# High and low parts of the activations interleaved in SBUF, and moved 256 bytes from the weights' place

## The chip, the cores and the metric

The kernel runs on one core of one Trainium2 chip. The metric is the device time of one execution in microseconds (us). A result here is the median of several executions, shown with the lowest and the highest. Beside them stands one profiled execution, in which the hardware recorded when each instruction began. Its records are read through views: a page with the totals, groups of instructions by line of the kernel, a timeline, and sums over stretches of time.

Five engines work side by side and wait for each other through semaphores. TensorE multiplies (PE in the profile, and PEld for the loads of its stationary operand), VectorE is DVE, ScalarE is ACT, GpSimd is POOL, and SyncE (SP) issues most of the DMAs.

## What is computed

The reference is one decoder block over 256 tokens with a model width of 2048, in float32:

```python
xn = _rms_norm(h, mix_norm_w[l])
proj = xn @ w_in[l]
p_ssm, p_gdn, p_gate = jnp.split(proj, [SSM_PROJ, SSM_PROJ + GDN_PROJ], axis=-1)
y_ssm = _ssd_branch(p_ssm, ...) @ w_branch_ssm[l]
y_gdn = _gdn_branch(p_gdn, ...) @ w_branch_gdn[l]
gates = jax.nn.sigmoid(p_gate.reshape(b_, t, N_BRANCHES, D_MODEL) + gate_b[l])
mixed = gates[:, :, 0] * y_ssm + gates[:, :, 1] * y_gdn
h = h + mixed @ w_out[l]
hn = _rms_norm(h, ffn_norm_w[l])
h = h + _peer_ffn(hn, peer_w_q[l], peer_sub_keys[l], peer_u[l], peer_v[l])
return _rms_norm(h, final_norm_w)
```

The two mixers are a Mamba-2 scan (ssm) and a gated delta net (gdn). The last sub-layer scores 16,384 single-neuron experts and keeps 16 for each of 8 heads. The kernel evaluates all the experts and weights them with a gate that is zero for those not chosen.

## The kernel before

All the large products have one form. The activations are the **stationary** operand (128 rows of the inner dimension by 128 tokens) and the weights are the **moving** operand (128 rows by mostly 512 columns). To keep float32 accuracy, each operand is cut into a high part in the type float32r and a low part that holds the rest. One product is then three matmuls: high by high, high by low, and low by high.

**The weights.** `Stream` loads 512 KB units (`raw`, 128 x 1024 floats, four buffers of 4096 bytes a partition) through SyncE. `split` (lines 100 to 111) cuts a unit with one activation on ACT (`whi`, line 107) and one subtraction on DVE (`wlo`, line 108), with three buffers each of 4096 bytes. There are 1129 units, used in a fixed order.

**The products.** `product` (lines 291 to 308) walks over the inner chunks k of a unit and the two token blocks tb. For each it issues lines 302, 303 and 304: `xa` by `h_`, `xa` by `l_`, `xb` by `h_`, where `xa` and `xb` are the high and the low part of the activations. After each k, `bg.step` may emit a step of a background chain (convolutions, scans, transposes, gates) between the matmuls. `mixing` (lines 1015 to 1027) does the same for the expert values, with lines 1021, 1022, 1027 and 1024.

**The activations.** They stand in these tiles, where a high and a low tile have the same shape:

- `xh`, `xl` (lines 243, 244): the normed input, for the input projection;
- `yh`, `yl` (lines 526, 624): the output of a mixer, for the branch projections;
- `mh`, `ml` (lines 729, 730): the merged branches, for the output projection;
- `hh`, `hl` (lines 788, 789): the second normed input, for the query product and the expert activations;
- `cf` (line 1009): the coefficients of the experts, for the mixing of the values, in two halves that are refilled in turn by `coef` (lines 990 to 996).

`split_t` (lines 248 to 250) writes a high part on ACT and the low part on DVE. In every one of these tiles the 256 tokens of a chunk are contiguous, so that a stationary operand reads 128 neighbouring floats (512 bytes) on each partition.

**The place in memory.** The pool `act` has four slots of 16,384 bytes on each partition, named `t16`, in which `xs`, `xh`, `xl`, `accg`, `aux`, `accs`, `h`, `hh`, `hl`, `keys`, the gate stages, `cf` and `fw` follow one another. Right behind it lie the four raw buffers, and behind them the three of `whi` and the three of `wlo`. Then come the pools of the stages, of which the last, `peer`, holds two `m16` slots: first `mh` and `ml`, later the two gate tiles `gg`.

Of the kernel before, what the change touches and what calls it, by code (L numbers as in the profile page):

```python
# [8 lines left out]
F = mybir.dt.float32  # L9
# [20 lines left out]
def in_proj_tiles():  # L30
    """Column ranges of w_in for each streamed tile, in the order in which they are used."""
    z, xs, b, c = 0, 4096, 8192, 9216
    dt = 10240
    gq, gk, gv = GDN_BASE, GDN_BASE + 2048, GDN_BASE + 4096
    gz = GDN_BASE + 8192
    bt = GDN_BASE + 12288

    def bc(g):
        return [(b + 128 * g, 128), (c + 128 * g, 128)]

    t = {"small": bc(0) + [(dt, 64), (bt, 16), (bt + 16, 16)]}
    for h in range(NH):
        t["qkv", h] = [(gq + 128 * h, 128), (gk + 128 * h, 128), (gv + 256 * h, 256)]
    for j in range(NH // 2):
        t["gz", j] = [(gz + 512 * j, 512)]
    for g in range(NG):
        t["sx", g] = [(xs + 512 * g, 512)]
        t["sz", g] = [(z + 512 * g, 512)]
    for g in (1, 3, 5):
        t["bc", g] = bc(g) + bc(g + 1)  # L50
    t["bc", 7] = bc(7)
    for i in range(2):
        for n in range(4):
            t["gate", i, n] = [(GATE_BASE + 2048 * i + 512 * n, 512)]
    return t


def schedule():
    """The order in which the weight tiles of the mixing sub-layer are used."""
    o = [("in", ("gz", 0)), ("in", "small")]  # L60
    for j in range(NH // 2):
        o.append(("in", ("qkv", 2 * j)))
        if j > 1:
            o.append(("br", "gdn", j - 2))
        o.append(("in", ("qkv", 2 * j + 1)))
        if j != 6:
            o.append(("in", ("gz", min(j + 1, 7))))
    o += [("in", ("gate", 1, 0)), ("in", ("gate", 1, 1)), ("br", "gdn", NH // 2 - 2),
          ("in", ("gate", 1, 2)), ("br", "gdn", NH // 2 - 1)]
    for g in range(NG):  # L70
        if g % 2:
            o.append(("in", ("bc", g)))
        o += [("in", ("sx", g)), ("in", ("sz", g))]
        if g:
            o.append(("br", "ssm", g - 1))
    o += [("in", ("gate", 1, 3)), ("in", ("gate", 0, 0)), ("in", ("gate", 0, 1)),
          ("br", "ssm", NG - 1), ("in", ("gate", 0, 2)), ("in", ("gate", 0, 3))]
    return o


class Stream:
    """Weights from DRAM: raw units ahead of their use, each cut into two float32r parts."""

# [37 lines left out]
class Background:  # L121
    """Chains of small steps that run between the large products."""

# [35 lines left out]
def block(ctx, tc, nc, I, out, dbg=None):  # L159
    cp = ctx.enter_context(tc.tile_pool(name="consts", bufs=1))  # L160
    T16 = ctx.enter_context(tc.tile_pool(name="act", bufs=4))
    big = ctx.enter_context(tc.tile_pool(name="big", bufs=4, space=PSUM))
# [3 lines left out]

# [1 line left out]
    order = schedule()  # L168
# [25 lines left out]

# [1 line left out]
    def big_tile():  # L196
# [20 lines left out]

    xs = T16.tile([128, 2, D], F, name="t16")
    strm = Stream(tc, nc, ctx, units, 4, 3)
# [15 lines left out]

# [1 line left out]
    def row_scale(r, m, parts):  # L237
        """m = sum of squares / D + eps, r = m ** -1/2, [128, 2] each"""
        V.tensor_reduce(m, parts, axis=mybir.AxisListType.X, op=OP.add)
        V.tensor_scalar(m, m, 1.0 / D, EPS, op0=OP.mult, op1=OP.add)  # L240
        power(r, m, 0, 2)

    xh = T16.tile([128, 16, T], FR, name="t16")
    xl = T16.tile([128, 16, T], FR, name="t16")
    sqp = cp.tile([128, 2, 4], F, name="sqp")
# [43 lines left out]

# [1 line left out]
    def product(lhs, nk, w, kpu, hook=None):  # L291
        """per token block, in PSUM: the sum over k chunks of lhs(k, tb) x streamed weights"""
        ps = [big_tile() for _ in range(2)]
        for u in range(nk // kpu):
            hi, lo = strm.next()
            for a in range(kpu):
                k = u * kpu + a
                h_, l_ = hi[:, a * w:(a + 1) * w], lo[:, a * w:(a + 1) * w]
                for tb in range(2):
                    xa, xb = lhs(k, tb)  # L300
                    o = ps[tb][:, :w]
                    PE.matmul(o, xa, h_, start=k == 0, stop=False)  # L302
                    PE.matmul(o, xa, l_, start=False, stop=False)  # L303
                    PE.matmul(o, xb, h_, start=False, stop=k == nk - 1)  # L304
                if hook:
                    hook(k)
                bg.step(1)
        return ps
# [3 lines left out]

# [1 line left out]
    raw0 = cp.tile([128, 2, 352], F, name="raw0")  # L314
# [8 lines left out]
    def small_gen():  # L323
# [10 lines left out]
        V.tensor_scalar(beta, beta, 0.5, 0.5, op0=OP.mult, op1=OP.add)  # L334
        # log(1 + e) = 2 atanh(e / (2 + e))
        V.tensor_scalar(s_, e_, 2.0, None, op0=OP.add)
# [29 lines left out]

# [1 line left out]
    mix = ExitStack()  # L368

    def conv(items, w, bias):  # L370
        """items of (dst, src psum [128, 256], chunk); dst gets half the causal convolution (+ bias)"""
        for dst, src, c in items:
            S.activation(dst, src, AF.Identity, scale=w[:, c, 3:4], bias=0.0 if bias is None else bias[:, c:c + 1])  # L373
        for k in (2, 1, 0):
            s = 3 - k
            for dst, src, c in items:
                V.scalar_tensor_tensor(dst[:, s:], src[:, :T - s], w[:, c, k:k + 1], dst[:, s:], op0=OP.mult, op1=OP.add)  # L377

    def conv_silu(pool, src, nch, chunk_of, w, bias, dst):
        """src(tb, i) [128 t, 128 c] in SBUF; dst [128 c, nch, 256] = silu(conv)"""  # L380
        y = pool.tile([128, 4, T], F, name="t4", bufs=NT4[0])
# [15 lines left out]
    def gdn_gen(h, pt, zg, yref):  # L397
# [127 lines left out]
        if not yref:  # L525
            yref += [mx.tile([128, 4, T], FR, name=n, bufs=1) for n in ("yh", "yl")]
        yh, yl = yref
# [15 lines left out]
    def ssm_gen(g, pt, bce, zg, yref):  # L543
# [78 lines left out]
        while g and ("ssm", g - 1) not in merged:  # L622
            yield
        yref += [mx.tile([128, 4, T], FR, name=n, bufs=1) for n in ("yh", "yl")]
        yh, yl = yref
# [97 lines left out]
    for o in order:  # L723
        if o[0] == "br":
            branch(o[1], o[2])
            if o[1:] == ("ssm", NG - 1):
                mix.close()
                pp = ctx.enter_context(tc.tile_pool(name="peer", bufs=1))
                mh = pp.tile([128, 16, T], FR, name="m16", bufs=2)
                ml = pp.tile([128, 16, T], FR, name="m16", bufs=2)  # L730
            continue
# [53 lines left out]

# [1 line left out]
    h = T16.tile([128, 2, D], F, name="t16")  # L787
    hh = T16.tile([128, 16, T], FR, name="t16")
    hl = T16.tile([128, 16, T], FR, name="t16")
    sqh = cp.tile([128, 2, 4], F, name="sqh")  # L790
# [36 lines left out]

# [1 line left out]
    tv, i1f, i2f = (pp.tile([128, 2, 8, 16], F, name=n) for n in ("tv", "i1f", "i2f"))  # L829
# [132 lines left out]

# [1 line left out]
    def act_gen(u, ps):  # L964
# [13 lines left out]

# [1 line left out]
    def gate_load(qg, half):  # L980
        ks = slice(16 * half, 16 * half + 16)
        src = gdr[ks, :, qg * 16:qg * 16 + 16, :].rearrange("k p i t -> p k i t")
        S.dma_start(gg[qg % 2][:, ks], src)

# [5 lines left out]
    def coef(qd, hq):  # L990
        g_ = gg[(qd // 4) % 2][:, :, (qd % 4) * 4:(qd % 4) * 4 + 4, :].rearrange("p k i t -> p i k t")
        h4 = hq.rearrange("p i (k t) -> p i k t", k=32)
        V.tensor_tensor(h4, h4, g_, op=OP.mult)
        hi, lo = cf[:, 0, qd % 2], cf[:, 1, qd % 2]
        S.activation(hi, hq, AF.Copy)
        V.tensor_tensor(lo, hq, hi.bitcast(F), op=OP.subtract)

    for u in range(32):
        if u == 31:
            bg.drain([ge])  # L1000
            gg = [pp.tile([128, 32, 16, 8], F, name="m16", bufs=2) for _ in range(2)]
            gate_load(0, 0)
# [5 lines left out]
        if u == 30:  # L1008
            cf = T16.tile([128, 2, 2, 4, T], FR, name="t16")
    acc = [[big_tile() for _ in range(2)] for _ in range(2)]  # L1010
# [4 lines left out]
    def mixing(i2, hv, cut, tb):  # L1015
        hi, lo = cut
        a, b = (cf[:, s, (i2 // 4) % 2, i2 % 4, tb * 128:(tb + 1) * 128] for s in range(2))
        for n in range(2):
# [33 lines left out]
    for i2, hv in v_order:  # L1052
        qd = i2 // 4
        if hv == 0:
# [6 lines left out]
            if i2 == 120:  # L1061
                fw = T16.tile([128, D], F, name="t16")
                G.dma_start(fw, bc_ap(I["fnw"], D))
# [15 lines left out]

# [1 line left out]
    residual(1, 0)  # L1081
# [77 lines left out]
```

## Time and profile before

| what | value |
|---|---|
| median of 3 runs | 3481.92 us (3481.53 to 3482.91) |
| span of the profiled execution, first to last instruction | 3480.8 us |
| PE busy | 3449.5 us (99%), 16598 matmuls |
| PEld busy | 2849.9 us (82%), 16598 loads |
| DVE busy | 2308.9 us (66%) |
| ACT busy | 1762.0 us (51%) |
| POOL busy | 318.3 us (9%) |
| moved by DMA | 682.36 MB, 196 GB/s in the mean |

The page gives the profiled execution by its span; it has no separate time with what lies around it, and the span is 1.1 us under the median. PE counts as busy from the start of a matmul to its modelled end. Matmuls overlap one another, so how fast PE works is read from the distance between starts, not from the busy share or from the length of one matmul.

### The profile page before, as it was taken

Reading aid. Unit: us, or ns where it says so; the run is one execution under the profiler, and the core shown is the slowest. Engines: PE = TensorE matmul, PEld = TensorE weight load, DVE = VectorE, ACT = ScalarE, POOL = GpSimd, SP = SyncE. Lnnn points to the kernel's source line nnn. Section 1 sums busy time; section 2 is a strip of 40 time slices with the busy share of each in tenths; the row PEclk is TensorE's granted clock in tenths of the full one; section 3 lists DMA queues with packets and bytes.
Section 4 is the critical chain, followed back from the end, with each engine's and each line's share of the span. In section 5 each row is a group of like instructions: output and inputs, shape, how many; then the busy total and the mean of one; then the engine's idle time right before and its main releaser. Section 6 shows DMA issues by size and latency. Waiting matters only on the chain.

```text
span 3480.8 us, 44496 instructions
## 1 busy us (share of the span) xinstructions
PE 3449.5 (99%) x16598; PEld 2849.9 (82%) x16598; DVE 2308.9 (66%) x3262; ACT 1762.0 (51%) x2420; POOL 318.3 (9%) x262
## 2 busy tenths in 40 slices
PE   9999999999999999999999999999999999999998
PEld 7888888888878888888888888888888788888886
DVE  6675766666667677777665667768887455555555
ACT  5565555555445554544445444446666444444444
POOL 0111111111100000000000000003443000000000
PEclk9999999999999999999999999999999999999999
DMA  7544444544555555555566566666777777777774
GB/s 258 158 138 152 151 145 142 154 150 147 157 166 183 192 187 182 185 178 182 189 203 200 172 199 208 206 210 224 236 241 242 253 245 242 241 242 243 241 234 163
DMA packets 233720, 682.36 MB, mean 196 GB/s; under 512 B 21072, under 2 KB 72480, under 8 KB 233248
## 3 DMA queue, kind: packets, MB, share of 16 engines
q1 hardware_dynamic: 164960, 594.03, 53.7%
q10 hardware_dynamic: 67616, 81.31, 6.8%
q0 software_dynamic: 928, 4.19, 0.4%
q8 instruction: 130, 2.13, 0.3%
q14 instruction: 86, 0.70, 0.1%
HBM read 643.71 MB, written 35.73 MB: 195 GB/s over the span
## 4 chain that ended last, share of the span: by engine, by line
PE 69%; DVE 1%; ACT 1%; issue 0%; ACTq 0%; DMA 0%; POOL 0%; POOLq 0%; DVEq 0%
PE acc L302 15%; PE acc L304 15%; PE acc L303 15%; PE acc L1022 3%; PE acc L1021 3%; PE acc L1027 3%; PE pst L1027 3%; PE pst L1021 3%; PE pst L1022 3%; PE pst L234 2%; PE pst L948 1%; PE pst L594 1%; DVE wlo L108 0%; ACT whi L107 0%; PE pst L598 0%
## 5 line engine op out<-in xcount | busy, mean ns | idle before, releaser
L108 DVE TENSOR_TENSOR wlo<-raw,whi 128x1024 fp32r<-128x1024 f32 (+1 forms) x1129 | 1439.9, 1282 | 916.2 <-ACT whi L107 906.1
L107 ACT ACTIVATE whi<-raw 128x1024 fp32r<-128x1024 f32 (+1 forms) x1129 | 1184.9, 1053 | 850.9 <-PE acc L304 440.5
L302 PE MATMUL acc<-whi,t 128*128 128x512 f32 (+2 forms) x2848 | 1168.8, 410 | 9.7 <-ACT whi L107 9.7
L304 PE MATMUL acc<-whi,t 128*128 128x512 f32 (+2 forms) x2848 | 1110.3, 390 | 0.0
L303 PE MATMUL acc<-wlo,t 128*128 128x512 f32 (+2 forms) x2848 | 1108.0, 389 | 1.8 <-DVE wlo L108 1.8
L304 PEld LDWEIGHTS acc<-whi,t 128*128 128x128 f32 x2848 | 535.6, 188 | 115.7
L302 PEld LDWEIGHTS acc<-whi,t 128*128 128x128 f32 x2848 | 536.7, 188 | 105.1 <-ACT whi L107 10.2
L303 PEld LDWEIGHTS acc<-wlo,t 128*128 128x128 f32 x2848 | 537.6, 189 | 99.2 <-DVE wlo L108 3.9
L302 PE MATMUL acc<-whi,yh 128*128 128x512 f32 x512 | 216.8, 423 | 2.8 <-ACT yh L249 2.8
L304 PE MATMUL acc<-whi,yl 128*128 128x512 f32 x512 | 202.9, 396 | 0.0
L303 PE MATMUL acc<-wlo,yh 128*128 128x512 f32 x512 | 202.4, 395 | 0.0
L1022 PE MATMUL pst<-wlo,t 128*128 128x512 f32 x512 | 200.0, 391 | 2.1 <-DVE wlo L108 2.1
L1021 PE MATMUL pst<-whi,t 128*128 128x512 f32 x512 | 200.1, 391 | 0.0
L1021 PE MATMUL acc<-whi,t 128*128 128x512 f32 x512 | 199.2, 389 | 0.0
L1022 PE MATMUL acc<-wlo,t 128*128 128x512 f32 x512 | 199.2, 389 | 0.0
L931 POOL TENSOR_TENSOR b<-ob,gp 128x1024 f16<-128x1024 f16 x64 | 141.0, 2203 | 625.6 <-DVE ob L930 625.6
L1027 PE MATMUL pst<-whi,t 128*128 128x512 f32 x508 | 156.8, 390 | 0.0
L1027 PE MATMUL acc<-whi,t 128*128 128x512 f32 x508 | 156.4, 389 | 0.0
L377 DVE SCALAR_TENSOR_TENSOR t<-pst,cols,t 128x255 f32<-128x255 f32 x336 | 135.9, 474 | 23.7 <-ACT t L373 23.3
L302 PEld LDWEIGHTS acc<-whi,yh 128*128 128x128 f32 x512 | 96.8, 189 | 23.2 <-ACT yh L249 3.2
L304 PEld LDWEIGHTS acc<-whi,yl 128*128 128x128 f32 x512 | 96.5, 188 | 23.3 <-DVE yl L250 0.2
L1022 PEld LDWEIGHTS pst<-wlo,t 128*128 128x128 f32 x512 | 96.5, 188 | 22.5 <-DVE wlo L108 2.4
(267 smaller groups left out, 3325.8 us busy)
## 6 DMA issues: line engine op xcount, KB each, us to landing
raw<-w_in SPq DMA_DIRECT2D x408, 512.0 KB, 3.6
raw<-u SPq DMA_DIRECT2D x256, 512.0 KB, 4.0
raw<-v SPq DMA_DIRECT2D x256, 512.0 KB, 4.4
raw<-w_gdn SPq DMA_DIRECT2D x64, 512.0 KB, 3.5
raw<-w_ssm SPq DMA_DIRECT2D x64, 512.0 KB, 4.4
raw<-w_out SPq DMA_DIRECT2D x32, 512.0 KB, 3.8
raw<-w_q SPq DMA_DIRECT2D x32, 512.0 KB, 3.6
hdr<-ht ACTq DMA_DIRECT2D x32, 512.0 KB, 4.9
```

The source lines that it names most:

```text
L107: self.nc.scalar.activation(hi[:, s], t[:, s], AF.Copy)
L108: self.nc.vector.tensor_tensor(lo[:, s], t[:, s], hi[:, s].bitcast(F), op=OP.subtract)
L234: PE.transpose(dst, src, ident)
L302: PE.matmul(o, xa, h_, start=k == 0, stop=False)
L303: PE.matmul(o, xa, l_, start=False, stop=False)
L304: PE.matmul(o, xb, h_, start=False, stop=k == nk - 1)
L377: V.scalar_tensor_tensor(dst[:, s:], src[:, :T - s], w[:, c, k:k + 1], dst[:, s:], op0=OP.mult, op1=OP.add)
L594: PE.matmul(p[:, i * 64:(i + 1) * 64], sc[:, i, :], xdt[:, c, i, :], start=True, stop=True)
L931: G.tensor_tensor(b2, ob[:, None, :, :].to_broadcast([128, 2, 4, 128]), gp[:, :, ts, None].to_broadcast([128, 2, 4, 128]), op=OP.mult)
L1021: PE.matmul(o_, a, hi[:, s], start=i2 == 0, stop=False)
L1022: PE.matmul(o_, a, lo[:, s], start=False, stop=False)
L1027: PE.matmul(acc[tb][2 * hv + n], b, hi[:, n * 512:(n + 1) * 512], start=False, stop=False)
```

## The change

The high and the low part of an activation no longer have a tile each. They share one, in which element 2t is the high part of token t and element 2t + 1 the low part. A stationary operand so reads 128 floats with a step of two, over 1024 bytes. `parts` gives the two views.

The pool `act` now has two `t16` slots and one larger tile, `pair`, for `xh`/`xl`, later `hh`/`hl`, and at the end `fw`. `pair` is 64 floats (256 bytes) longer than its contents, and `xs` makes the two `t16` slots 16 floats (64 bytes) longer each. The products, the order of the work and the number of instructions are as before. Docstrings and comments that the diff also removes are left out here.

```diff
-    T16 = ctx.enter_context(tc.tile_pool(name="act", bufs=4))
+    T16 = ctx.enter_context(tc.tile_pool(name="act", bufs=2))
+
+    def pair_tile(dt):
+
+        t = T16.tile([128, 2 * 16 * T + 64], dt, name="pair", bufs=1)
+        return t
+
+    def parts(t, k):
+        t = t[:, :2 * k * T].rearrange("p (k t s) -> p k t s", k=k, s=2)
+        return t[:, :, :, 0], t[:, :, :, 1]
+
...
-    xs = T16.tile([128, 2, D], F, name="t16")
+    xs = T16.tile([128, 2 * D + 16], F, name="t16")[:, :2 * D].rearrange("p (a b) -> p a b", a=2)
...
-    xh = T16.tile([128, 16, T], FR, name="t16")
-    xl = T16.tile([128, 16, T], FR, name="t16")
+    xh, xl = parts(pair_tile(FR), 16)
...
-            yref += [mx.tile([128, 4, T], FR, name=n, bufs=1) for n in ("yh", "yl")]
+            yref += parts(mx.tile([128, 8 * T], FR, name="yhl", bufs=1), 4)
...
-                mh = pp.tile([128, 16, T], FR, name="m16", bufs=2)
-                ml = pp.tile([128, 16, T], FR, name="m16", bufs=2)
+                mh, ml = parts(pp.tile([128, 32 * T], FR, name="m32"), 16)
...
-    hh = T16.tile([128, 16, T], FR, name="t16")
-    hl = T16.tile([128, 16, T], FR, name="t16")
+    hh, hl = parts(pair_tile(FR), 16)
...
-        S.dma_start(gg[qg % 2][:, ks], src)
+        S.dma_start(gg[:, qg % 2, ks], src)
...
-        hi, lo = cf[:, 0, qd % 2], cf[:, 1, qd % 2]
+        hi, lo = (c[:, 4 * (qd % 2):4 * (qd % 2) + 4] for c in cf)
...
-            gg = [pp.tile([128, 32, 16, 8], F, name="m16", bufs=2) for _ in range(2)]
+            gg = pp.tile([128, 2, 32, 16, 8], F, name="m32")
...
-            cf = T16.tile([128, 2, 2, 4, T], FR, name="t16")
+            cf = parts(T16.tile([128, 16 * T], FR, name="t16"), 8)
...
-        a, b = (cf[:, s, (i2 // 4) % 2, i2 % 4, tb * 128:(tb + 1) * 128] for s in range(2))
+        a, b = (c[:, i2 % 8, tb * 128:(tb + 1) * 128] for c in cf)
...
-                fw = T16.tile([128, D], F, name="t16")
+                fw = pair_tile(F)[:, :D]
```

More of the change, by code (lines that the diff above doesn't have):

```diff
@@ L623, in ssm_gen @@
             yield
-        yref += [mx.tile([128, 4, T], FR, name=n, bufs=1) for n in ("yh", "yl")]
+        yref += parts(mx.tile([128, 8 * T], FR, name="yhl", bufs=1), 4)
         yh, yl = yref
@@ L990, in coef @@
     def coef(qd, hq):
-        g_ = gg[(qd // 4) % 2][:, :, (qd % 4) * 4:(qd % 4) * 4 + 4, :].rearrange("p k i t -> p i k t")
+        g_ = gg[:, (qd // 4) % 2, :, (qd % 4) * 4:(qd % 4) * 4 + 4, :].rearrange("p k i t -> p i k t")
         h4 = hq.rearrange("p i (k t) -> p i k t", k=32)
         V.tensor_tensor(h4, h4, g_, op=OP.mult)
-        hi, lo = cf[:, 0, qd % 2], cf[:, 1, qd % 2]
+        hi, lo = (c[:, 4 * (qd % 2):4 * (qd % 2) + 4] for c in cf)
         S.activation(hi, hq, AF.Copy)
```

## The prediction

> **What bounds the kernel now.** The page comes first: the busy times, the slices, and the chain that ended last.
>
> ```profile
> span 3480.8 us, 44496 instructions
> ...
> PE 3449.5 (99%) x16598; PEld 2849.9 (82%) x16598; DVE 2308.9 (66%) x3262; ACT 1762.0 (51%) x2420; POOL 318.3 (9%) x262
> ...
> PE   9999999999999999999999999999999999999998
> ...
> PEclk9999999999999999999999999999999999999999
> ...
> PE 69%; DVE 1%; ACT 1%; issue 0%; ACTq 0%; DMA 0%; POOL 0%; POOLq 0%; DVEq 0%
> ```
>
> PE is full in every slice at a full clock, and the chain is PE's. So only the pace of the matmuls matters. The groups by line and shape say how many there are.
>
> ```profile
> L302 PE MATMUL acc<-whi,t 128*128 128x512 f32 x2784 | 1149.1, 413 | 9.7 <-ACT whi L107 9.7
> ...
> L302 PE MATMUL acc<-whi,yh 128*128 128x512 f32 x512 | 216.8, 423 | 2.8 <-ACT yh L249 2.8
> ...
> L302 PE MATMUL acc<-whi,m 128*128 128x512 f32 x128 | 50.7, 396 | 0.0
> ```
>
> Lines 303 and 304 go with 302, so 512-column matmuls number 3 x 2784 = 8352 on `xh`/`xl` and `hh`/`hl`, 3 x 512 = 1536 on `yh`/`yl`, and 3 x 128 = 384 on `mh`/`ml`. The mixing adds 256 units of 12, which is 3072 on `cf`. In all 13344. Idle time before them is about ten us, so the rest is pace. The timeline gives it: the first and the last of the 96 matmuls of the 352-column product, then of the 96 of the last branch product, then two pairs of plain float32 matmuls, and a group of four.
>
> ```profile
> 30.49 0.32 PE L302 MATMUL acc<-whi,t 128*128 128x352 f32 x1
> ...
> 45.71 0.32 PE L304 MATMUL acc<-whi,t 128*128 128x352 f32 x1
> ...
> 1737.73 0.40 PE L302 MATMUL acc<-whi,yh 128*128 128x512 f32 x1
> ...
> 1759.90 0.39 PE L304 MATMUL acc<-whi,yl 128*128 128x512 f32 x1
> ```
> ```profile
> 189.34 0.59 PE L499 MATMUL pst<-st,cT 128*128 128x256 f32 x2
> 189.77 0.59 PE L500 MATMUL pst<-st,cT 128*128 128x256 f32 x2
> ...
> 800.06 0.60 PE L478 MATMUL pst<-xx,mm 128*128 128x128 f32 x4
> ```
>
> The sums over stretches (start:end, length, PE busy and count first) give the same for long undisturbed runs on `xh`/`xl` and in the mixing.
>
> ```profile
> 1702.00:1736.00 34.00, 34.00 (x152) 28.15 (x151) 17.56 (x16) 15.45 (x16) 0.54 (x1) 1.00 0.67 210
> ...
> 2780.00:3460.00 680.00, 680.00 (x3002) 563.06 (x3001) 371.94 (x312) 294.37 (x284) 0.34 (x1) 1.00 0.72 236
> ```
>
> A matmul of 0.39 us that starts every 0.227 us overlaps the edges of a stretch 1.7 times, so the mixing starts one each 680 / 3000.3 = **226.6 ns**, and the x product one each 34 / 150.3 = 226 ns. The 352-column ones come each 15.22 / 95 = 160.2 ns. The difference, 66.4 ns for 160 columns, is 0.415 ns a column. Then 512 columns are 212.5 ns, and **14 ns are left over on each matmul**, whatever its width (352 columns: 146.1 + 14.1). On `yh`/`yl` the distance is 22.17 / 95 = 233.4 ns, with 21 left over.
>
> The float32 pairs lack the 14 ns. Two passes of 256 columns start 0.43 us before the next two, so 215 ns each. That is two column times a column, 212.5, and 2.5 left over. Their stationary operand is loaded beside the matmul before, and the load is as long:
>
> ```profile
> 2768.16 0.39 PE L303 MATMUL acc<-wlo,t 128*128 128x512 f32 x1
> 2768.16 0.19 PEld L304 LDWEIGHTS acc<-whi,t 128*128 128x128 f32 x1
> ```
>
> By groups, the loads of both kinds and the matmuls of line 478 (count, busy us, mean ns of one):
>
> ```profile
> L304 PEld LDWEIGHTS acc<-whi,t 128*128 128x128 f32 x2848 | 535.6, 188 | 115.7
> ...
> L478 PE MATMUL pst<-xx,mm 128*128 128x128 f32 x384 | 58.4, 274 | 0.0
> L478 PEld LDWEIGHTS pst<-xx,mm 128*128 128x128 f32 x384 | 57.8, 190 | 8.2
> ```
>
> So a load starts with the matmul before it. My reading is that both read SBUF, and that the float32r matmul, which takes a float every 0.415 ns, is held up by the load beside it; the float32 one takes a float every 0.83 ns and has room. Two things speak for contention rather than a fixed price of float32r: the left-over is per load and not per column, and it differs with the place. By the sizes of the tiles, every stationary start in `act` and `m16` lies a multiple of 512 bytes from the moving start (14 ns); in the ssm pool `yh` and `yl` lie 64 bytes past such a multiple (21 ns).
>
> **The change part by part.** *Step of two.* The four in the row of line 478 start (600 - 274) / 3 = 109 ns apart, so a load delivers 128 columns in 109 ns or less, one each 0.85 ns. With 4 bytes a column the load walks at half the matmul's speed of 4 bytes in 0.415 ns, and the two addresses slide over each other, meeting and parting. With 8 bytes a column both walk at the same speed, so a distance once free of collisions stays free. *256 bytes.* Behind `pair` (33,024 bytes) come four raw buffers of 4096, so `whi` begins 49,408 = 96 x 512 + 256 bytes behind it. `wlo`, the other buffers, chunks and token blocks add multiples of 512. So 8352 matmuls have the new distance. `cf` stands in a `t16` slot of 16,448 bytes, 128 or 192 bytes past a multiple of 512; `m32` stands at 0; `yhl` stays at 64 in ssm.
>
> *The price of one.* No row shows a strided stationary read beside a float32r matmul. The lower end is the float32 pair's left-over, 2.5 ns: 226.6 becomes 215. The upper end, if every 16 bytes that the load reads cost as much as now, is 28 ns: 240.5. I take 215 for `pair` and `cf`, because in lockstep they resemble most the float32 pair, whose matmul and load also walk at one speed. The sum: 8352 x 11.6 = 97 us, and 3072 x 11.6 = 36 us. For `m32` (no distance) and `yhl` (place as before) I count nothing, with bounds of 384 x 11.6 + 1536 x 18.4 = 33 us gained and 384 x 14 = 5 us lost.
>
> *The loads themselves.* They may take 188 ns or, read twice as wide, up to 376. At 109 ns of throughput there is room to 218 before they set the pace, so up to a doubling they cost 3 ns at most, 40 us; I take nothing.
>
> [...]
>
> *The strided writes.* ACT and DVE now write `split_t`'s and `coef`'s outputs in steps of 8 bytes.
>
> ```profile
> L950 ACT ACTIVATE t<-pst 128x512 f32<-128x512 f32 x64 | 78.0, 1220 | 68.4 <-PE pst L948 68.4
> L996 DVE TENSOR_TENSOR t<-p,t 128x1024 fp32r<-128x1024 f32 x32 | 39.2, 1227 | 36.0 <-ACT t L995 36.0
> L975 ACT ACTIVATE ht<-pst 128x512 f32<-128x512 f32 x64 | 38.2, 599 | 70.8 <-PE pst L234 70.7
> L995 ACT ACTIVATE t<-p 128x1024 fp32r<-128x1024 f32 x32 | 33.9, 1060 | 76.7 <-DVE p L993 76.7
> ...
> L250 DVE SCALAR_TENSOR_TENSOR yl<-pst,cols,yh 128x256 fp32r<-128x256 f32 x64 | 30.8, 481 | 24.2 <-ACT yh L249 24.2
> L249 ACT ACTIVATE yh<-pst,cols 128x256 fp32r<-128x256 f32 x64 | 30.3, 473 | 63.0 <-DVE yl L250 42.8 <-PE pst L234 20.2
> ```
>
> Line 950 writes in steps of 32 bytes and takes 1220 ns where line 975 takes 599 contiguously. So a strided write costs between nothing and double; 8 bytes are nearer to nothing. Doubled, all `split_t` and `coef` add about 0.5 us x 100 on each engine and 1.1 us x 32, some 85 us each on engines that are 51% and 66% busy beside a full PE. It is exposed where PE waits for them: twice before the first matmul and once before the mixing, some 3 us. I count 1 us. Shared tiles may also make a matmul on the high part wait for the low one (481 ns) at the start of a product; that is under the same 3 us.
>
> *What is late next.* In the gate stage, PE at a quicker pace meets a DVE that has little room.
>
> ```profile
> 2370.00:2680.00 310.00, 310.00 (x1769) 248.34 (x1768) 264.97 (x221) 200.05 (x210) 139.10 (x63) 1.00 0.71 237
> ```
>
> DVE works 265 of 310 us. At 5% less time it is 90% busy, and the cuts of line 108 wait behind the gate steps. I count 3 us lost, at most the stage's own gain of about 13. DMA moves at most 5% more a second; its share there is 0.71, so it fits.
>
> The sum is 97 + 36 - 1 - 3 = 129 us off 3480.8, which is 1.1 us under the median: about **3352**, given as 3350. With `yhl` and `m32` gaining too it is 3318; with `cf` gaining nothing, 3388.
>
> **The rivals.** *The left-over is float32r's own.* Then nothing moves: 3482, give or take 5. Against it stands the 233.4 of the branch product, where only the stationary's place differs; for it, that no 512-column float32r matmul shows less than 14.
>
> [...]
>
> *Only the place counts, and the new one is a bad one.* If a distance off the multiples of 512 costs 21 as on `yh`, 8352 + 3072 matmuls lose 6.8 ns each: 78 us, **3560**. It decides as soon as the x product's distance rises above 226.6.
>
> *Each 16 bytes of stationary read costs the same.* 512 bytes are 32 times 16, and 14 ns are about 32 column times. Twice the bytes then give 28 ns: 13344 x 14 = 187 us, 3669. Against it: `yh` pays 21 for the same bytes.
>
> *A partial gain.* If half of the collisions stay, 11424 x 5.8 = 66 us go, to 3416.
>
> **How the numbers follow.** My forecast (3315 to 3395) has 0.64; the partial gain (to 3475) 0.12; nothing changed 0.08; the bad place 0.09; the price by bytes 0.07. That makes faster 0.76, same 0.08, slower 0.16, where 0.2% (7 us) is about what a measurement of this kernel tells from no change. The range goes from 3310, under the full gain, to 3488, over the unchanged time: it leaves out the slower rivals, 0.16.
>
> **What would show it.** In the new profile, starts on `xh`, `hh` and `cf` 215 to 218 ns apart, and 149 for 352 columns, show the lockstep; 226.6 shows that the left-over is float32r's own; 233 the bad place; 240 the bytes. Loads still near 188 ns show that the step is free; line 995 near 1060 that the strided writes are. Idle time of PE behind line 108 in the gate stage would show DVE as the next bound. The forecast is wrong if collisions depend on something that walking in step does not fix, or if the matmuls' 14 ns is a fixed price.

## The result and the profile after

| | before | after |
|---|---|---|
| median | 3482.41 us (3481.53 to 3484.06, 4 runs) | 3532.17 us (3532.05 to 3532.43, 4 runs) |
| ratio of the times | | 1.0144, 95% interval 1.013 to 1.0158 |
| span of the profiled execution | 3480.8 us | 3530.5 us |

The change made the kernel 1.4% **slower**. The forecast was 3350 us, and the time lies outside its range. The page of the kernel after, with the span, the busy times, the granted clock and the shares of the chain:

```profile
span 3530.5 us, 44496 instructions
...
PE 3502.6 (99%) x16598; PEld 2942.4 (83%) x16598; DVE 2306.5 (65%) x3262; ACT 1766.4 (50%) x2420; POOL 299.4 (8%) x262
...
PEclk9999999999999999999999999999999999999999
...
PE 97%; DVE 1%; ACT 1%; issue 0%; DMA 0%; ACTq 0%; POOL 0%; POOLq 0%; SPq 0%; DVEq 0%
```

The number of instructions, the clock and the bound are those of before. The span grew by 50 us and PE's busy time by 53 us, as longer distances between the starts of its matmuls. The same two stretches as before (an `xh`/`xl` product, then the mixing) and the gate stage between them:

```profile
1715.00:1750.00 35.00, 35.00 (x152) 29.40 (x151) 17.43 (x17) 15.16 (x15) 0.54 (x1) 1.00 0.65 204
...
2370.00:2680.00 310.00, 310.00 (x1713) 253.22 (x1713) 255.49 (x233) 194.45 (x205) 114.93 (x59) 1.00 0.70 229
2785.00:3500.00 715.00, 715.00 (x3087) 604.07 (x3086) 384.01 (x321) 306.06 (x294) 0.61 (x1) 1.00 0.72 236
```

Counted as in the prediction, the x product starts a matmul each 35 / 150.3 = 233 ns (226 before) and the mixing each 715 / 3085.3 = 231.7 ns (226.6 before). The last stretch begins 19 us ahead of the mixing; by the starts of the mixing's own matmuls it is 231.4 ns. The timeline gives the first and the last of 96 matmuls of the 352-column product, of 96 of the last branch product, and of 76 on the merged branches:

```profile
31.11 0.32 PE L311 MATMUL acc<-whi,pair 128*128 128x352 f32 x1
...
46.36 0.32 PE L313 MATMUL acc<-whi,pair 128*128 128x352 f32 x1
...
1751.30 0.40 PE L311 MATMUL acc<-whi,yhl 128*128 128x512 f32 x1
...
1773.47 0.39 PE L313 MATMUL acc<-whi,yhl 128*128 128x512 f32 x1
...
1876.20 0.40 PE L312 MATMUL acc<-wlo,m 128*128 128x512 f32 x1
...
1893.87 0.40 PE L312 MATMUL acc<-wlo,m 128*128 128x512 f32 x1
```

That is 15.25 / 95 = 160.5 ns at 352 columns, where nothing changed (160.2), 22.17 / 95 = 233.4 ns on `yhl`, exactly as before at the same place, and 17.67 / 75 = 235.6 ns on `m32`. In the groups by line, the loads:

```profile
L313 PEld LDWEIGHTS acc<-whi,pair 128*128 128x128 f32 x2848 | 554.1, 195 | 109.4
```

A load with a step of two takes 195 ns instead of 188. The whole difference can be put down to the tiles by adding up, over the trace, the distance from each float32r matmul's start to the next matmul's start (this includes the few small matmuls between them):

| stationary tile | matmuls | before, us | after, us | difference |
|---|---|---|---|---|
| `xh`, `xl`, `hh`, `hl` (352 and 256 columns too) | 8544 | 2009.8 | 2047.5 | +37.7 |
| `cf` | 3072 | 700.5 | 714.9 | +14.4 |
| `mh`, `ml` | 384 | 89.0 | 91.3 | +2.4 |
| `yh`, `yl` | 1536 | 376.7 | 372.8 | -4.0 |

Together +50.5 us, close to the 49.7 us of the span. So the time came from the pace of the float32r matmuls alone, where the prediction looked, with the sign reversed.

### The profile page after: what moved, and what is told of

Read it like the earlier page. It is cut to its first block, busy times and chain, and to the rows that moved or that the text cites. A ratio compares the mean times of both kernels' runs of the same rounds, so it can differ in the third digit from the quotient of the medians.

```text
span 3530.5 us, 44496 instructions
## 1 busy us (share of the span) xinstructions
PE 3502.6 (99%) x16598; PEld 2942.4 (83%) x16598; DVE 2306.5 (65%) x3262; ACT 1766.4 (50%) x2420; POOL 299.4 (8%) x262
## 4 chain that ended last, share of the span: by engine, by line
PE 97%; DVE 1%; ACT 1%; issue 0%; DMA 0%; ACTq 0%; POOL 0%; POOLq 0%; SPq 0%; DVEq 0%
PE acc L311 23%; PE acc L312 22%; PE acc L313 22%; PE pst L244 3%; PE acc L1028 3%; PE acc L1029 3%; PE acc L1034 3%; PE pst L1028 3%; PE pst L1029 3%; PE pst L1034 3%; PE pst L479 1%; PE pst L487 1%; PE pst L955 1%; PE pst L603 1%; DVE wlo L108 1%
## 5 line engine op out<-in xcount | busy, mean ns | idle before, releaser
L311 PE MATMUL acc<-whi,pair 128*128 128x512 f32 (+2 forms) x2848 | 1181.3, 415 | 8.4 <-ACT whi L107 8.4
L312 PE MATMUL acc<-wlo,pair 128*128 128x512 f32 (+2 forms) x2848 | 1119.8, 393 | 1.3 <-DVE wlo L108 1.3
L313 PE MATMUL acc<-whi,pair 128*128 128x512 f32 (+2 forms) x2848 | 1119.2, 393 | 0.0
L313 PEld LDWEIGHTS acc<-whi,pair 128*128 128x128 f32 x2848 | 554.1, 195 | 109.4
L311 PEld LDWEIGHTS acc<-whi,pair 128*128 128x128 f32 x2848 | 555.7, 195 | 99.6 <-ACT whi L107 8.8
L312 PEld LDWEIGHTS acc<-wlo,pair 128*128 128x128 f32 x2848 | 555.3, 195 | 93.1 <-DVE wlo L108 3.3
L311 PE MATMUL acc<-whi,yhl 128*128 128x512 f32 x512 | 216.0, 422 | 2.1 <-ACT yhl L258 2.1
L312 PE MATMUL acc<-wlo,yhl 128*128 128x512 f32 x512 | 201.6, 394 | 0.0
L313 PE MATMUL acc<-whi,yhl 128*128 128x512 f32 x512 | 201.4, 393 | 0.0
L938 POOL TENSOR_TENSOR b<-ob,gp 128x1024 f16<-128x1024 f16 x64 | 124.4, 1944 | 656.9 <-DVE ob L937 653.3
L1028 PEld LDWEIGHTS pst<-whi,t 128*128 128x128 f32 x512 | 100.4, 196 | 18.7 <-ACT whi L107 0.3
L311 PEld LDWEIGHTS acc<-whi,yhl 128*128 128x128 f32 x512 | 100.0, 195 | 19.2 <-ACT yhl L258 2.5
```

The lines of the kernel that those rows point to most:

```text
L938: G.tensor_tensor(b2, ob[:, None, :, :].to_broadcast([128, 2, 4, 128]), gp[:, :, ts, None].to_broadcast([128, 2, 4, 128]), op=OP.mult)
L1028: PE.matmul(o_, a, hi[:, s], start=i2 == 0, stop=False)
```

## The experiments

Theory A after the result: the **step** of two costs, wherever the operand lies. Rival B: the new **place**, 256 bytes off, costs. Behind both stood a third question: whether the 14 ns are a collision with the load at all, as the prediction had read them. Below, "distance" is the time from one matmul's start to the next. A mean over a stretch is its length over the count less 1.7. "By the starts" means that the distances in the trace were averaged one by one.

### e1: the place alone

```diff
+        self.pad = ctx.enter_context(tc.tile_pool(name="pad", bufs=1)).tile([128, 64], F, name="pad")
+        nc.gpsimd.memset(self.pad, 0.0)
```

These lines stand in `Stream` of the kernel before, ahead of the weights' pools. They put 256 bytes between the contiguous activations and the weights.

> The kernel before with the weights moved 256 bytes further and nothing else, so that every stationary operand of xh, xl, hh, hl and cf still reads neighbouring floats but stands 256 bytes past a multiple of 512 from the weights. If the place is what costs, the matmuls on them start 233 ns apart instead of 226.7, and the time is near 3482 + 11424 x 6.7 ns = 3559 us. If the step of two is what costs, they stay at 226.7 and the time at 3482.

Measured: 3482.11 us (10 runs) beside 3482.48 (13 runs), ratio 0.9999 (0.9989 to 1.0008). The mixing:

```profile
2785.00:3385.00 600.00, 600.00 (x2649) 496.99 (x2648) 330.08 (x276) 259.00 (x248) 0.00 (x0) 1.00 0.73 242
```

600 / 2647.3 = 226.6 ns, as before. A place 256 bytes off costs a contiguous operand nothing, and brings nothing. B falls.

### e2: the step alone

```diff
-        t = T16.tile([128, 2 * 16 * T + 64], dt, name="pair", bufs=1)
+        t = T16.tile([128, 2 * 16 * T], dt, name="pair", bufs=1)
...
-    xs = T16.tile([128, 2 * D + 16], F, name="t16")[:, :2 * D].rearrange("p (a b) -> p a b", a=2)
+    xs = T16.tile([128, 2, D], F, name="t16")
```

This is the kernel after without its two pads.

> The changed kernel without its two paddings: the step of two stays, and the stationary operands stand at multiples of 512 bytes from the weights again. If the place is what costs, the matmuls on the pair tile and on cf start 226.7 ns apart and the time is near 3482, or less because yhl gained. If the step costs, they are at 233 or more: the tile m32 of the changed kernel stood at distance 0 with the step of two and showed 235.5, which would give 3482 + 11424 x 8.8 ns = 3582 us.

Measured: 3540.14 us (3537.01 to 3541.19, 4 runs), ratio 1.0164 (1.0147 to 1.0181). The mixing:

```profile
2800.00:3380.00 580.00, 580.00 (x2492) 480.63 (x2491) 312.49 (x261) 248.80 (x238) 0.61 (x1) 1.00 0.73 238
```

580 / 2490.3 = 232.9 ns (233.3 by the starts). Summed by tile as above, `xh` to `hl` cost 39.9 us more than before and `cf` 20.2 more, with `mh` and `yh` as in the kernel after. So the step costs 58 us by itself. The 3582 us of the expectation were too many: `cf` lost 20.2 us / 3072 = 6.6 ns a matmul, not 8.8, and `xh` to `hl`, many of whose matmuls were slow before, 39.9 us / 8544 = 4.7. The pads of the change give 8 us back, mostly on `cf`, whose place they also change. A stands.

### e3 and e4: all places, with a step of one and of two

Each chunk of 256 tokens got a pitch 32 bytes longer than its contents, so that the 16 chunks of `xh`, `xl`, `hh` and `hl` stand at different places against the weights; `hh` and `hl` start 16 bytes further on. The core of e3, in the kernel before (e4 does the same to the kernel of e2):

```diff
-    xh = T16.tile([128, 16, T], FR, name="t16")
-    xl = T16.tile([128, 16, T], FR, name="t16")
+    def chunks(o):
+        t = T16.tile([128, 16 * (T + 8)], FR, name="t16")
+        return t[:, o:o + 15 * (T + 8) + T], T + 8
+
+    class Chunks:
+        def __init__(self, o):
+            self.t, self.p = chunks(o)
+
+        def __getitem__(self, i):
+            _, k, s = i
+            s0, s1 = (s.start or 0), (T if s.stop is None else s.stop)
+            return self.t[:, k * self.p + s0:k * self.p + s1]
+
+    xh = Chunks(0)
+    xl = Chunks(0)
...
-    hh = T16.tile([128, 16, T], FR, name="t16")
-    hl = T16.tile([128, 16, T], FR, name="t16")
+    hh = Chunks(4)
+    hl = Chunks(4)
```

> The kernel before with 32 bytes more between the chunks of xh, xl, hh and hl, and hh, hl a further 16 bytes on: chunk k of the input projection stands 32 k bytes past a multiple of 512 from the weights, chunk k of the query product and the expert activations 32 k + 16. If only the distance modulo 512 counts, the starts of chunk 0 are 226.7 ns apart, those of chunk 2 (64 bytes) 233, those of chunk 8 (256) 233, and the curve may show distances under 226.7. If some other thing set 233 on yh, all the chunks show 226.7.

> The changed kernel without its paddings and with 32 bytes more between the chunks of the pair tile, 16 bytes further for hh and hl: the same distances with the step of two. If the place counts alone, the curve over the chunks is that of the contiguous sweep. If the step in lockstep makes it all or nothing, as the prediction had it, some distances show 215 and others far more than 233. If the step costs by its bytes, all show 233 to 240.

Measured: e3 3505.94 us and e4 3531.36 us (one run each). In e1 a place 256 bytes on had made no difference (226.6 ns), so the places are taken by their bytes past a multiple of 256. The means of the distances in ns by the place of the operand that is loaded meanwhile, from the starts in the trace, without those over 260 ns:

```text
bytes past a multiple of 256     0     16     32     48     64     96    128    160    192    224    240
e3, step of one              230.9  229.9  233.1  233.1  233.2  232.9  232.4  233.7  230.7  233.3  229.1
e4, step of two              232.6  233.3  231.1  231.2  230.3  233.2  231.7  233.6  233.4  233.8  231.2
```

The means hold matmuls near background steps, which come at 228 to 240 ns; in the kernel before, 2931 of 11,423 distances on `t16` tiles lie there and some 7900 at 224 to 227. All but some 70 of the 2931 are the last distance ahead of a group of background matmuls or among the first eleven behind one. In the timeline of the kernel before, a background group, the second large matmul behind it, the eleventh, and the one 12 further on:

```profile
2101.12 0.60 PE L234 MATMUL pst<-cst,p 128*128 128x128 f32 x4
...
2101.79 0.40 PE L303 MATMUL acc<-wlo,t 128*128 128x512 f32 x1
...
2103.88 0.39 PE L303 MATMUL acc<-wlo,t 128*128 128x512 f32 x1
...
2106.60 0.39 PE L303 MATMUL acc<-wlo,t 128*128 128x512 f32 x1
```

The distance is 2.09 / 9 = 232 ns at first and 2.72 / 12 = 226.7 ns then: the contiguous operand takes some ten matmuls to settle at its pace. The sweeps change the place every 6 matmuls. Their means are therefore not the settled pace of a place (at 0, a step of one has 230.9 here and 226.7 in the kernel before); they show which places disturb more and which less.

Over six matmuls in a row on `xh` to `hl`, the quickest mean is 226.7 ns in e3 and 229.2 in e4. One stretch of the query product, of the kernel before, of e3 and of e4 (small matmuls count here too, so only the three are to be compared):

```profile
1910.00:2330.00 420.00, 420.00 (x1953) 348.14 (x1952) 298.09 (x673) 203.65 (x230) 0.00 (x0) 1.00 0.64 199
```
```profile
1920.00:2340.00 420.00, 420.00 (x1920) 343.29 (x1919) 294.04 (x665) 200.43 (x226) 0.17 (x1) 1.00 0.62 196
```
```profile
1940.00:2360.00 420.00, 420.00 (x1920) 354.10 (x1920) 296.77 (x676) 200.73 (x226) 0.00 (x0) 1.00 0.63 196
```

33 matmuls fewer in 420 us, 1.7%, both with a step of one at mixed places and with a step of two. Summed by tile, `xh` to `hl` cost 24.5 us more than before in e3, 30.0 in e4 and 39.9 in e2. So a step of one loses most of what the step of two loses, as soon as it leaves the multiples of 256 bytes. A step of two has better and worse places in the sweep (64 has the least, 230.3 ns), but none that looks free, as walking in step should give.

### e5 and e6: a shorter load

Do the 14 ns come from the load? In the mixing of the kernel before (e5) and of e2 (e6) the stationary operand loses half or three quarters of its columns, while the matmul keeps its 512:

```diff
+        m = 128 if i2 in (0, 127) else (64, 32)[hv]
+        a, b = a[:, :m], b[:, :m]
...
-            o_ = acc[tb][2 * hv + n]
+            o_ = acc[tb][2 * hv + n][:m]
```

> The kernel before, whose mixing (apart from its first and last row of experts) uses 64 of the 128 tokens of a block for the even units and 32 for the odd ones; the output lacks the rest. The moving operand stays at 512 columns. If the 14 ns left over on each matmul come from the load beside it, they shrink with it: starts about 220 ns apart with 64 columns and 216 with 32, and the mixing ends some 25 us earlier. If they are a fixed price of a float32r matmul, all stay at 226.7.

> The same cut of the mixing in the kernel with the step of two and no paddings, where full loads gave 233.3. If the extra 6.7 ns of the step go with the bytes that the load reads, they halve with 64 columns and fall to a quarter with 32: about 230 and 228 over a fixed 226.7, or 223 and 218 if all 20 ns go with the load. If they are paid once a matmul, 233.3 stays.

Measured: e5 3495.87 us and e6 3519.63 us (one run each). The load of 64 columns in the groups of e5, and the mixing there, in two views:

```profile
L1023 PEld LDWEIGHTS acc<-whi,t 128*64 128x64 f32 x504 | 68.2, 135 | 52.3
```
```profile
2785.00:3385.00 600.00, 600.00 (x2605) 316.40 (x2603) 324.88 (x271) 255.59 (x244) 0.00 (x0) 1.00 0.73 238
```

The loads are shorter (135 ns instead of 188; PEld is busy 316 of 600 us instead of 497), yet the matmuls come each 600 / 2603.3 = 230.5 ns, **later** than with the full load; the mixing took 11.6 us more, not 25 less. By the starts it is 229.0 ns with 64 columns and 231.7 with 32. In e6:

```profile
2785.00:3385.00 600.00, 599.62 (x2636) 329.99 (x2637) 330.55 (x277) 261.54 (x254) 0.61 (x1) 0.99 0.75 246
```

599.62 / 2634.3 = 227.6 ns over the stretch, which begins 20 us ahead of the mixing. By the starts of the mixing's own matmuls it is 226.8 ns with 64 and 226.9 with 32 columns, where e2 had 233.3. So a shorter load takes away all that the step added, and nothing below. The 14 ns do not shrink with the load. The reading of the prediction falls here, and the 7 ns above it prove to be the part that depends on the load.

Three limits belong to this. The matmul with fewer columns loaded also writes fewer rows of its result. In e5 the two widths alternate every 12 matmuls, about the time that PE took to settle behind background matmuls (some ten), so 229.0 and 231.7 need not be settled paces. And every matmul still has a load: a price paid once for each load, however short, would look the same, and no run has two matmuls on one load.

### e7 and e10: a narrower matmul

At 352 columns the step cost nothing (160.5 ns beside 160.2). To see where that begins, the mixing was narrowed to 480 and 384 columns in the kernel of e2 (e7), and then with contiguous operands in the kernel before (e10):

```diff
-            o_ = acc[tb][2 * hv + n]
-            s = slice(n * 512, (n + 1) * 512)
+            w = 512 if i2 == 0 else (480, 384)[hv]
+            o_ = acc[tb][2 * hv + n][:, :w]
+            s = slice(n * 512, n * 512 + w)
```

> The kernel with the step of two and no paddings, whose mixing (apart from its first row of experts) uses 480 of 512 columns for the even units and 384 for the odd ones; the output lacks the rest. The 352-column product showed no extra with the step of two (160.5 ns against 160.2). If the extra is a collision of the load with the moving reads it must stay whenever the load fits beside the matmul: 220 ns and 180 ns apart. If it is bound to the full 512 columns, it goes: 213.3 and 173.3.

> The kernel before with the mixing cut to 480 columns in the even and 384 in the odd units as in the run with the step of two, which showed 216.6 and 173.8 ns. If 13.3 ns are the fixed price of a float32r matmul, the contiguous one shows 213.3 and 173.3, so that the step's extra is 3.3 at 480 columns and 0.4 at 384. If the extra had gone for another reason, the contiguous one falls by as much.

Measured: e7 3439.47 us, e10 3402.84 us (one run each). The timelines, first of e7, then of e10, from the start of six matmuls of 480 columns to that of the next six, of 384, and on:

```profile
2901.72 0.38 PE L1029 MATMUL acc<-whi,t 128*128 128x480 f32 x1
...
2903.02 0.34 PE L1029 MATMUL pst<-whi,t 128*128 128x384 f32 x1
...
2904.06 0.34 PE L1029 MATMUL pst<-whi,t 128*128 128x384 f32 x1
```
```profile
2901.15 0.38 PE L1022 MATMUL acc<-whi,t 128*128 128x480 f32 x1
...
2902.45 0.34 PE L1022 MATMUL pst<-whi,t 128*128 128x384 f32 x1
...
2903.50 0.33 PE L1022 MATMUL pst<-whi,t 128*128 128x384 f32 x1
```

Six take 1.30 and 1.04 us in e7, 1.30 and 1.05 in e10. Over the whole mixing, by the starts, the distances are 216.6 and 173.8 ns with a step of two, 216.5 and 173.9 contiguous. At 480 and 384 columns **the step is free**. And at 480 both have 216.5 - 480 x 0.415 = 17 ns left over, not 14. So, of the widths tried, only the full 512 pays for the step, and there the contiguous operand at a multiple of 256 bytes is a special case that fits.

### e8: `yh` and `yl` put at a multiple of 256 bytes

If that special case is what before has, then `yh` and `yl`, which miss it, should gain from it. A pad of 32 floats (gated delta net) and of 48 (scan) ahead of `yh`, contiguous as before, moves both tiles there:

```diff
+    def y_tiles(pad):
+        a = mx.tile([128, 4 * T + pad], FR, name="yh", bufs=1)[:, pad:].rearrange("p (k t) -> p k t", k=4)
+        return [a, mx.tile([128, 4, T], FR, name="yl", bufs=1)]
...
-            yref += [mx.tile([128, 4, T], FR, name=n, bufs=1) for n in ("yh", "yl")]
+            yref += y_tiles(32)
...
-        yref += [mx.tile([128, 4, T], FR, name=n, bufs=1) for n in ("yh", "yl")]
+        yref += y_tiles(48)
```

> The kernel before with 128 and 192 bytes ahead of yh, so that yh and yl too stand at a multiple of 256 bytes from the weights, with neighbouring floats as before. If the sweep's optimum (226.7 ns at multiples of 256) holds for them, the 1536 branch matmuls start 227 instead of 233 ns apart, and the time falls by 1536 x 6.4 ns = 10 us to 3472. If something else about the branch products makes them slow, nothing changes.

Measured: **3476.91 us** (3474.13 to 3480.71, 11 runs) beside 3482.29, ratio 0.9986 (0.9977 to 0.9995). The last branch product in the timeline:

```profile
1732.47 0.39 PE L302 MATMUL acc<-whi,yh 128*128 128x512 f32 x1
...
1754.01 0.39 PE L304 MATMUL acc<-whi,yl 128*128 128x512 f32 x1
```

21.54 / 95 = 226.7 ns, where before had 233.4. The sum over `yh` and `yl` falls by 5.3 us, which is the whole gain and half of the 10 us expected. This version beats both kernels, if by little: by the starts, 816 of the 1536 distances now lie under 228 ns (20 before), while the others, most of them near background matmuls, gain less than 6.7 ns each or nothing.

### e9: a step of four

The kernel before with the `y` operands interleaved by four in the gated delta net and by two in the scan, the high part at the place of e8:

```diff
+        s = 4 if pad == 32 else 2
+        a = mx.tile([128, 4 * T * s + pad], FR, name="yhl", bufs=1)[:, pad:].rearrange("p (k t s) -> p k t s", k=4, s=s)
+        return [a[:, :, :, 0], a[:, :, :, 1]]
```

> The kernel before, whose yh and yl stand at a multiple of 256 bytes from the weights as in the run with y in place (226.7 ns there with neighbouring floats), but with a step of four floats in the gdn half of the branch products and of two in the ssm half. If the step costs by the 16-byte pieces of SBUF that a load touches (32, 64 and 128 for steps of one, two and four), the ssm products show about 233 as the step of two did elsewhere and the gdn ones 245 or more. If a step merely takes the load out of an exact fit, both show 230 to 236.

Measured: 3494.84 us (one run). In the timeline, 73 matmuls with a step of four and 96 with a step of two:

```profile
1009.44 0.40 PE L304 MATMUL acc<-whi,yhl 128*128 128x512 f32 x1
...
1026.36 0.39 PE L304 MATMUL acc<-whi,yhl 128*128 128x512 f32 x1
...
1750.13 0.39 PE L302 MATMUL acc<-whi,yhl 128*128 128x512 f32 x1
...
1772.30 0.40 PE L304 MATMUL acc<-whi,yhl 128*128 128x512 f32 x1
```

16.92 / 72 = 235.0 ns and 22.17 / 95 = 233.4 ns. Twice as many bytes passed over cost 1.6 ns more, where a price by 16-byte pieces, which was an assumption, asked for 12 or more. That rival falls. The load itself does grow with a step of four, as the records on `yhl` from 1000 to 1030 us show (least, median and greatest ns):

```profile
L304 PEld LDWEIGHTS acc<-whi,yhl x31: 307/310/334, 999.9 to 1026.1; 128*128 128x128 f32 x31
```

It takes 310 ns, where the step of two takes 193 in the last branch product of this run and a step of one 188. So a load 117 ns longer goes with 1.6 ns more a matmul, and one 5 ns longer with 6.7: the price does not follow the length of the load.

### e11: the step on `cf` alone

```diff
-            cf = T16.tile([128, 2, 2, 4, T], FR, name="t16")
+            cf = T16.tile([128, 16 * T], FR, name="t16").rearrange("p (k t s) -> p k t s", k=8, s=2)
+            cf = cf[:, :, :, 0], cf[:, :, :, 1]
```

In the kernel before; the lines of `coef` and `mixing` follow as in the change.

> The kernel before with cf alone interleaved, at a multiple of 512 bytes from the weights. If the step is what costs, the mixing's matmuls start 233.3 ns apart as in the run with the step alone, and the time rises by 3072 x 6.7 ns = 20 us to 3503, with every other stage as before. If the loss came from sharing a tile or from the strided writes of ACT and DVE, PE would show waits in front of the mixing's matmuls instead and the distance would stay 226.7.

Measured: 3502.10 us (3500.94 to 3503.39, 4 runs), ratio 1.006 (1.0044 to 1.0077). The mixing, and line 995:

```profile
2785.00:3385.00 600.00, 600.00 (x2573) 496.39 (x2572) 321.23 (x268) 255.07 (x242) 0.00 (x0) 1.00 0.72 234
```
```profile
L995 ACT ACTIVATE t<-p 128x1024 fp32r<-128x1024 f32 x32 | 36.4, 1136 | 76.7 <-DVE p L993 76.7
```

600 / 2571.3 = 233.3 ns. 3072 x 6.7 ns = 20.6 us, which is the added time within its spread; by the trace's starts the mixing grew 20.2 us and no other tile's sum moved by more than 1.4. So the pace explains it without any other cost: the price is per matmul and adds up.

One thing always comes with the step in these runs: the low part stands 4 bytes behind the high, so it is no longer at a multiple of 256 bytes. No run has a contiguous operand 4 bytes off, or a step with the low part in place. Here the distance is 233.2 to 233.4 ns whether the high or the low part is loaded meanwhile, which speaks for the step without excluding the 4 bytes.

### e12: everything 64 bytes further on

```diff
-    half = cp.tile([128, 2], F, name="half")
+    half = cp.tile([128, 18], F, name="half")
```

In the kernel before, the first pool grows by 64 bytes, so that all activations and weights move together.

> The kernel before with every tile from the first on 64 bytes further, so that all distances between stationary operands and weights stay as they were. If the distance decides, the mixing's matmuls start 226.7 ns apart and the branch products' 233.4 as before, and the time is 3482. If the absolute address decides, the pace of the stages changes, with the mixing up to 233 and the time up to 3560.

Measured: 3481.9 us beside 3479.35 (one run each). The mixing:

```profile
2785.00:3385.00 600.00, 600.00 (x2649) 496.82 (x2648) 329.69 (x276) 259.30 (x248) 0.00 (x0) 1.00 0.74 242
```

600 / 2647.3 = 226.6 ns. With everything moved by these 64 bytes nothing changed in the mixing, while `yh` and `yl` fell from 233.4 to 226.7 ns when a pad moved them against the weights (e8): this speaks for the distance between the two operands, and against the place of either by itself.

## Why the prediction was wrong

**The bound was read rightly.** PE sets the time at a granted clock of 0.998, and the sum of the distances gives the difference within 1 us.

**The step that failed is "the price of one".** The prediction took the 14 ns for a collision of the matmul's reads with the load's, and so for something that the layout could take away: 226.6 ns to 215. The runs show two prices where it saw one. The first, 14 ns, is there with 128, 64 and 32 columns loaded (e5, e6), with steps of one, two and four, in every place of the sweeps, and at 512, 384, 352 and 256 columns of the matmul (226.7, 173.9, 160.2 and 120 ns contiguous, where the columns alone are 212.5, 159.4, 146.1 and 106.2); in no long stretch was it less. No layout tried here removes it; at the full clock it is a fixed price of a float32r matmul, or of the load that goes with each, as far as these runs go. The second, 0 to 9 ns on top (226.7 to 235.6 ns at 512 columns), does depend on the load: in e6 it went with the shorter one, from 233.3 to 226.8 ns, and in the other runs it varies with the step, the place and the width. The kernel before paid it only on `yh` and `yl` and near background matmuls, so there was little to gain (5.4 us in e8) and 7 ns a matmul to lose. In numbers: -97 us forecast on `xh` to `hl`, +37.7 measured; -36 on `cf`, +14.4.

**The argument for contention did not carry.** "The left-over is per load and not per column, and it differs with the place": each matmul here has one load, so a price per load and one per matmul look the same. And what differs with the place is the 7 ns, not the 14. The trace of before had a row that could have told this: the float16 matmuls of the gate stage, here a row of four, with a load for each one (512 of 98 ns in the mean).

```profile
2372.09 0.40 PE L948 MATMUL pst<-b,oa 128*128 128x128 f16 x4
...
L948 PE MATMUL pst<-b,oa 128*128 128x128 f16 x512 | 39.7, 220 | 0.0
```

(400 - 220) / 3 = 60 ns between starts, 55 to 56 by the unrounded ones, and 128 x 0.415 = 53 ns. With 2 to 3 ns over their columns they have no 14 ns. This speaks for a price of the type; half the bytes a column leave a little room for the other reading, which e5 and e6 narrow to a price that does not depend on the length of the load.

The traces show one thing more, for a few matmuls just behind a wait, where the granted clock was 0.50. First a stretch and two matmuls of the kernel before, six starts apart, then of the kernel after, nine starts apart:

```profile
2751.50:2754.40 2.90, 2.90 (x8) 2.18 (x7) 1.15 (x1) 0.00 (x0) 0.00 (x0) 0.50 1.02 410
...
2751.45 0.63 PE L304 MATMUL acc<-whi,t 128*128 128x512 f32 x1
...
2754.01 0.63 PE L304 MATMUL acc<-whi,t 128*128 128x512 f32 x1
```
```profile
2785.40:2788.90 3.50, 3.50 (x10) 2.73 (x9) 1.22 (x1) 0.00 (x0) 0.00 (x0) 0.50 1.03 412
...
2784.89 0.63 PE L313 MATMUL acc<-whi,pair 128*128 128x512 f32 x1
...
2788.73 0.63 PE L313 MATMUL acc<-whi,pair 128*128 128x512 f32 x1
```

2.56 / 6 and 3.84 / 9 are both 426.7 ns, and 512 columns at twice 0.415 ns are 425. At half the clock neither the 14 ns nor the 7 ns of the step are there, though a load, here of 0.33 us, still stands beside each matmul. So neither price is a fixed number of clock pulses, nor a time that is added at any clock.

**Lockstep** gave nothing: at 512 columns a step of two is not free at any place where it stood long enough to settle (230 to 235.6 ns on the tiles of the kernel after and of e2), nor does the sweep of e4 point to one.

**The place.** A contiguous operand 256 bytes past a multiple of 512 had 226.6 ns in e1, as one at the multiple has in the kernel before. So its 256 bytes count as no move, and `pair` had in this sense not moved at all.

**`m32` and `yhl`**, counted as nothing, gave +2.4 and -4.0 us. `m32` lost the fit (226.7 to 235.6 ns) as `pair` did (226.7 to 233.3); `yhl` had no fit to lose, and in the two stages together the step of two at its places came out a little better than the contiguous tiles.

**The rivals.** "The left-over is float32r's own" came nearest to the first price, and its 3482 failed only because the step costs up to 9 ns besides. The bad place met its mark, 233 ns on the x product, for the wrong reason: the mark was put on a number that a cost of the step gives too, and only e1 and e2 separate them. Its 78 us were also too many, because a quarter of the matmuls, those near background steps, already came at 228 ns or later, and because `cf` at its new place lost 14.4 us / 3072 = 4.7 ns each, not 6.8.

**What held.** The loads kept nearly their length (195 ns to 188). The strided writes are almost free and hidden, as these groups of the kernel after show beside 1060, 1227, 473 and 481 ns:

```profile
L1002 ACT ACTIVATE t<-p 128x1024 fp32r<-128x1024 f32 x32 | 36.0, 1125 | 76.7 <-DVE p L1000 76.7
L1003 DVE TENSOR_TENSOR t<-p,t 128x1024 fp32r<-128x1024 f32 x32 | 39.3, 1228 | 38.1 <-ACT t L1002 38.1
...
L258 ACT ACTIVATE yhl<-pst,cols 128x256 fp32r<-128x256 f32 x64 | 31.5, 492 | 62.4 <-DVE yhl L259 41.3 <-PE pst L244 21.0
L259 DVE SCALAR_TENSOR_TENSOR yhl<-pst,cols,yhl 128x256 fp32r<-128x256 f32 x64 | 30.8, 481 | 25.2 <-ACT yhl L258 25.1
```

ACT pays 6% and 4%, DVE nothing. No wait of PE came in its place; its longest in the waits of the kernel after (total us, count, longest) are:

```profile
PE acc L311 <- ACT whi L107: 8.4, 2, 6.0
PE pst L1029 <- DVE wlo L108: 2.1, 1, 2.1
PE acc L311 <- ACT yhl L258: 2.1, 1, 2.1
```

DVE as the next bound in the gate stage was not tested: PE came no quicker there, and DVE was busy 255 of 310 us.

**Still open** is how the 0 to 9 ns come about: why a contiguous operand at a multiple of 256 bytes pays none of them with 128 columns loaded (226.7 ns) and some with 64 and 32 (229.0 and 231.7 in e5), and why the shortened load with a step of two pays none (226.8 and 226.9 in e6). What the 14 ns are paid for, and why they go at half the clock, is open too. A rule for places and steps that fits all the rows was not found.

## What to carry to other kernels

Before a left-over per matmul is taken for contention, look in the same trace for matmuls with the same load but another type or width, and change one operand of one stage alone (e11, two lines) before relaying all of them. Try a float32r stationary operand contiguous, with its distance from the moving operand a multiple of 256 bytes: at 512 columns this was worth 6.7 ns a matmul here, on `cf` (233.3 in e11, 226.6 before) and on `yh` and `yl` (233.4 before, 226.7 in e8). A mark in a prediction is worth something only if no rival gives the same number.

## What was not expected of the hardware

- At the full clock, a float32r matmul of 512 columns never came quicker than 226.6 ns over an undisturbed stretch, whatever was done to the stationary operand: 512 x 0.415 and 14 more. At a granted clock of 0.50 it came each 426.7 ns, within 2 ns of its columns alone, and with a step of two just the same.
- Behind a group of background matmuls, a contiguous operand at a multiple of 256 bytes took some ten matmuls to settle at 226.7 ns.
- The same matmul at 480 columns, contiguous, takes 216.5 ns, 10 ns less for 32 columns (13 by the columns), and at 512 it loses 7 ns at once when the fit is gone. The undisturbed distances lie on few values: 226.7, 230, 231.4, 233.3, 235.6.
- A load of 128 columns took 188 ns with a step of one, 193 with two and 310 with four, while the matmuls beside it came each 226.7, 233.4 and 235.0 ns at multiples of 256 bytes.
- Loading fewer contiguous columns made the matmul slower: 226.6 ns with 128, 229.0 with 64, 231.7 with 32, where 64 and 32 alternated every 12 matmuls.
